# One pair of low matmuls behind the next six, in the down products and behind the mixer's totals

## The chip, the cores and the metric

One Trainium2 chip, one of its cores. The metric is the device time of one execution in microseconds (us); a median of three runs is given. TensorE is called PE, its weight loads PEld, VectorE DVE, ScalarE ACT, GpSimd POOL, and the queue that starts most loads SP.

## What is computed

One step of an encoder layer over T = 576 tokens (512 of a prompt and 64 of a running stream), with a model width of 1024 and an FFN width of 2816, all in fp32:

```python
x = x + 0.5 * swiglu_ffn(rms_norm(x, ffn1_norm), ffn1_w_gate_up, ffn1_w_down)
h = rms_norm(x, mix_norm)
p = h @ w_in                                  # 1024 -> 7168
y_a = (a_b * dwconv3(a_c * a_v)) @ w_a_out
y_b = silu(layer_norm(dwconv31(glu(b_u)) + bias)) @ w_b_out
x = x + (sigmoid(gate_a) * y_a + sigmoid(gate_b) * y_b) @ w_out
x = x + 0.5 * swiglu_ffn(rms_norm(x, ffn2_norm), ffn2_w_gate_up, ffn2_w_down)
y = rms_norm(x, final_norm)
```

The last inputs of the two convolutions are returned too.

## The kernel before

Features lie on the 128 partitions and the 576 tokens along the free dimension, so a product's output tile is 128 features by two halves of 288 tokens, each half in a PSUM bank of its own. Each fp32 operand is split into a high part (fp32r) and a low part, the rounded rest. A product of 128 input features (one *chunk*) is then three products, high x high, high x low, low x high, on two halves: six matmuls. `mm` (line 396) issues them in the order of `SIX`: four with the chunk's high weights (half 0, half 0, half 1, half 1), then two with its low weights (half 0, half 1). Each matmul comes with a weight load of 128x128.

```python
SIX = ((0, 0), (1, 0), (0, 1), (1, 1), (2, 0), (2, 1))

parts = ((whi, xh), (whi, xl), (wlo, xh))
```

Instructions of each engine are kept in the order in which the program issues them. Stages, in order:

- **First FFN.** Its 22 rows of gate and up tiles come in four groups of 5, 5, 6 and 6 (`GROUPS`). A first few rows are plain products; the others are *pairs* of seven *blocks* (`block`, line 417), each 12 matmuls into one bank. Behind each group stand its down products: eight output tiles `j`, each over the group's rows as chunks. Tiles 0 and 1 run together, chunk by chunk (`both`, line 470), tiles 2 to 7 one behind the other (`product`, line 444). In the last group `finish1` does this.
- **Mixer.** 56 products of `w_in` and 8 of `w_a_out`, `w_b_out` and `w_out` each, of 8 chunks (48 matmuls). Sums over features (RMSNorm, LayerNorm) are made by matmuls with a tile of ones: `Sum.total`, called a *total*, has four, a high and a low term on each half. There is one behind the mixer's first product, one for LayerNorm's mean, and one for its variance.
- **Second FFN.** As the first, with one total behind its first gate product. Of its last group only tiles 0 to 2 are made as above; tiles 3 to 7 (the *late* ones) are made over the first 304 tokens, then over the other 272, three matmuls a chunk.

Weights come in fp32 by SP. ACT rounds them to the high part, and a POOL DMA that adds makes the low part from the raw tile; for some tiles DVE subtracts instead. A weight tile's buffers come free when PE has used it.

The change adds a function `turn` beside `mm` and a flag `turned`, and touches `product`, `both` and `total`.

Of the kernel before, what the change touches and what calls it, by code (L numbers as in the profile page):

```python
# [56 lines left out]
SIX = ((0, 0), (1, 0), (0, 1), (1, 1), (2, 0), (2, 1))  # L57
# [49 lines left out]
def tile_encoder_step(  # L107
# [25 lines left out]
    def nm(s):  # L133
        uid[0] += 1
        return f"{s}_{uid[0]}"
# [16 lines left out]
    def psum2():  # L152
        return mmps.tile([P, 2, 512], F32, tag="mm", name=nm("mm"))
# [41 lines left out]
    class Stream:  # L195
# [91 lines left out]
        def lead(self, n, ahead=None):  # L287

            self.load_ahead()
            n, total = n + (ahead or self.ahead), len(self.units)  # L290
            while self.done < min(total, self.begun, n):
                self.end()
            while self.added < min(total, n + 2):
                self.add()
            while self.begun < min(total, n + 1):
                self.begin()
# [99 lines left out]
    def mm(ps, w, kk, xs, first, last, spans=HALVES, six=SIX):  # L396


        (whi, wlo), (xh, xl) = w, xs
        parts = ((whi, xh), (whi, xl), (wlo, xh))  # L400
        for n, s in six:
            if s < len(spans):
                (a, b), (i, e) = parts[n], spans[s]
                pe.matmul(
                    ps[:, s, : e - i], a[:, kk, :], b[:, i:e],
                    start=first and n == 0, stop=last and n == 2,
                )

    def chunks(name):

        got = []
        for n in plan[name]:
            w = ws.get(n)
            got += [(w, kk) for kk in range(ws.units[n][1])]
        return got

    def block(w, xs):
# [5 lines left out]
                pe.matmul(q, l[:, k, :], r, start=k == m == 0, stop=k == KU - 1 and m == 2)  # L423
        return q


    work = []

# [2 lines left out]
    def fill():  # L431
        while work and dve.time < pe.time - AHEAD:
            work.pop(0)()

    def take():

        while behind:
            ready, then = behind.pop(0)
            dve.time = max(dve.time, ready)
            then()  # L440
# [3 lines left out]
    def product(name, xs, then=None, order=None, got=None, soon=None):  # L444


        if name in early:
            return early.pop(name)[:, :, :H]
        ps = psum2()
        if order or got:  # L450
            got = got or chunks(name)
            for n, k in enumerate(order or range(len(xs))):
                mm(ps, *got[k], xs[k], n == 0, n == len(xs) - 1)
        else:
            k = 0
            for n in plan[name]:
                w = ws.get(n)
                for kk in range(ws.units[n][1]):
                    mm(ps, w, kk, xs[k], k == 0, k == len(xs) - 1)
                    k += 1  # L460
                    if soon and k == 1:
                        soon()
        take()
        if then is None:
            dve.time = max(dve.time, pe.time)
            return ps[:, :, :H]
        fill()
        behind.append((pe.time, lambda: then(ps[:, :, :H])))

    def both(names, xs):  # L470

        ps = [psum2() for _ in names]
        ws_ = [chunks(name) for name in names]
        for k in range(len(xs)):
            for p, w in zip(ps, ws_):
                mm(p, *w[k], xs[k], k == 0, k == len(xs) - 1)
        return [p[:, :, :H] for p in ps]
# [24 lines left out]
    class Sum:  # L502
# [49 lines left out]
        def total(self, spans=HALVES, room=None):  # L552

            if room:
                n = T // len(room)
                for s, out in enumerate(room):
                    for one, v in self.terms:
                        pe.matmul(
                            out, one, v[:, s * n : (s + 1) * n],
                            start=v is self.terms[0][1], stop=v is self.terms[-1][1],  # L560
                        )
                return room
            p = psum2()
            span = slice(spans[0][0], spans[-1][1])
            terms = self.terms or [(ones, self.acc[:, span]), (ones, self.last)]
            for s, (i, e) in enumerate(spans):
                for n, (one, v) in enumerate(terms):
                    pe.matmul(
                        p[:, s, : e - i], one, v[:, i - span.start : e - span.start],
                        start=n == 0, stop=n == 1,  # L570
                    )
            n = spans[0][1] - spans[0][0]
            return p[:, :, :n] if len(spans) == 2 else p[:, 0, :n]
# [190 lines left out]
    ws.ahead = 2  # L764
    name = ("f1", "u", 1)
    ps = product(name, xg, soon=root)
    early[name] = ps

# [10 lines left out]
    def ffn(f, xg, sums, finish, forms, R=None, todo=()):  # L779
# [5 lines left out]
        def plain(i, hs):  # L785
            nonlocal R
            t, up = ttile(), (f, "u", i)
            ps = product((f, "g", i), xg, order=IN_TURN if f == "f2" and i == 0 else None)
            got = None if up in early else chunks(up)
            if R is None:  # L790
                R = rstd(sums)
            ups = product(up, xg, got=got)
            hs.append(None)
            at = len(hs) - 1
# [73 lines left out]
        for g, grp in enumerate(GROUPS):  # L868
            hs = []
            for i in grp:  # L870
                if i < PLAIN[f]:
                    plain(i, hs)
                    continue
                if i == PLAIN[f]:
                    ws.ahead = AHEAD_UNITS
                    bs = forms.operands(xg)
                pair(i, hs, grp[-1] == FT - 1)
            while rest:
                rest.pop(0)()
            spare.clear()  # L880
            if grp[-1] < FT - 1:
                for j, ps in enumerate(both([(f, "d", g, j) for j in range(2)], hs)):
                    update(j, ps, R)
                for j in range(2, KT):
                    update(j, product((f, "d", g, j), hs), R)
            else:
                finish(g, hs)

    def finish1(g, hs):
        table(AF.Abs_reciprocal_sqrt)  # L890
        ps = both([("f1", "d", g, j) for j in range(2)], hs)
        for j in range(KT):
            update(j, ps[j] if j < 2 else product(("f1", "d", g, j), hs))
            nxg.append(split_scaled(X[j], par(j, R_NM)))
            nss.square(X[j])
            nss.add(dve)
# [115 lines left out]
    for j in range(KT):  # L1012
        raw = j < RAW_J
        xs = xg if raw else xn
# [142 lines left out]
    for j in range(KT):  # L1157
        ps = product(("yb", j), BA)
# [8 lines left out]
    for n, j in enumerate(IN_TURN):  # L1167
        ps = product(("o", j), MS)
# [4 lines left out]
        p = n // 2  # L1173
# [12 lines left out]
    def finish2(g, hs):  # L1186
        fsum = Sum()
        table(AF.Abs_reciprocal_sqrt)
        ps = both([("f2", "d", g, j) for j in range(2)], hs)
        for j in range(LATE[0]):  # L1190
            update(j, ps[j] if j < 2 else product(("f2", "d", g, j), hs))
# [121 lines left out]
```

## Time and profile before

| | us |
|---|---|
| median of three runs | 1294.79 |
| lowest, highest | 1294.35, 1294.93 |
| the profiled execution | 1294.93 |
| its span, first to last instruction | 1293.2 |
| PE busy in it | 1283.2 |

The profile is of one execution. A busy time is the union of instructions, and matmuls overlap: each lasts some 290 ns from start to modelled end, and the next starts some 130 ns after it did. A row of the timeline is a run of like instructions: its start, its length up to the end of the last, and how many; the start of the next row less its own start is the time that its matmuls took. Where a helper records every operation all have one line (L83), so stages are told apart by time and by names of tiles.

### The profile page before, as it was taken

What the parts mean: (1) busy time and instruction counts of PE and PEld (TensorE: products, weight loads), DVE (VectorE), ACT (ScalarE), POOL (GpSimd) and SP (SyncE); (2) the same over time, 40 slices, a digit from 0 to 9 for tenths busy, and PEclk for the clock granted to TensorE, in tenths of its full rate; (3) what the DMA queues carried; (4) which work ended last, traced back from release to release, by engine and by line L of the source; (5) the groups of instructions that cost most, each with busy time, mean ns of one, the idle gap of its engine ahead of it and who ended that gap; (6) DMA issues with size and microseconds to landing.
All of it is one profiled execution on the core that took longest, in us unless ns stands there. A gap on an engine that the chain in (4) does not pass through costs nothing.

```text
span 1293.2 us, 25663 instructions
## 1 busy us (share of the span) xinstructions
PE 1283.2 (99%) x9752; PEld 1281.8 (99%) x9752; DVE 893.0 (69%) x1477; ACT 763.5 (59%) x1353; POOL 370.2 (29%) x470
## 2 busy tenths in 40 slices
PE   9999999999999999999999999999999999999997
PEld 9999999999999999999999999999999999999997
DVE  6858668748846998898885160346857858847956
ACT  7646656645776655555454674467665655654664
POOL 0032322322333444333321322222142241241230
PEclk9999999999999999999999999999999999999999
DMA  7286786886799898787885978776697696796683
GB/s 223 66 187 150 164 183 148 178 178 152 153 196 186 172 204 167 171 170 171 175 170 121 206 158 167 168 158 140 139 176 175 149 197 148 160 209 135 160 173 93
DMA packets 285948, 213.16 MB, mean 165 GB/s; under 512 B 15360, under 2 KB 248832, under 8 KB 285824
## 3 DMA queue, kind: packets, MB, share of 16 engines
q0 software_dynamic: 57600, 95.05, 44.7%
q1 hardware_dynamic: 226480, 115.63, 31.4%
q8 instruction: 77, 1.26, 0.4%
q10 hardware_dynamic: 1744, 0.83, 0.2%
q14 instruction: 47, 0.39, 0.1%
HBM read 113.81 MB, written 2.62 MB: 90 GB/s over the span
## 4 chain that ended last, share of the span: by engine, by line
PE 88%; issue 8%; DMA 2%; POOL 1%; DVE 1%; ACT 0%; POOLq 0%; DVEq 0%; SPq 0%; ACTq 0%
PE mm L83 88%; DMA u<-raw 1%; POOL g L83 1%; POOL u L83 1%; DMA raw<-in_ffn_w_gate_up_dram 0%; DMA raw<-in_ffn_w_down_dram 0%; DMA g<-raw 0%; DVE g L83 0%; DVE tmp L83 0%; POOLq L83 0%; DVE w L83 0%; DVEq L1303 0%; ACT g L83 0%; ACT u L83 0%; DVE r L83 0%
## 5 line engine op out<-in xcount | busy, mean ns | idle before, releaser
L83 PE MATMUL mm<-act,u 128*128 128x288 f32 x4686 | 660.3, 293 | 0.2 <-DMA u<-raw 0.2
L83 PEld LDWEIGHTS mm<-act,u 128*128 128x128 f32 x4686 | 630.7, 188 | 0.4 <-DMA u<-raw 0.4
L83 PE MATMUL mm<-act,g 128*128 128x288 f32 x2778 | 399.2, 294 | 0.0
L83 PEld LDWEIGHTS mm<-act,g 128*128 128x128 f32 x2778 | 377.9, 188 | 0.0
L83 PE MATMUL mm<-act,act 128*128 128x288 f32 (+2 forms) x2244 | 306.1, 293 | 0.0
L83 PEld LDWEIGHTS mm<-act,act 128*128 128x128 f32 x2244 | 297.4, 188 | 0.3 <-ACT act L83 0.3
L83 POOL DMA_DIRECT2D u<-raw x197 | 171.7, 871 | 411.3 <-ACT u L83 300.8
L83 ACT CAST u<-raw 128x512 fp32r<-128x512 f32 (+2 forms) x203 | 116.2, 572 | 155.8 <-PE mm L83 127.3
L83 POOL DMA_DIRECT2D g<-raw x117 | 101.9, 871 | 274.4 <-ACT g L83 220.0
L83 DVE SCALAR_TENSOR_TENSOR w<-g,prm,w 128x606 f32<-128x606 f32 x232 | 179.2, 842 | 1.4 <-ACT w L83 1.4
L83 DVE TENSOR_TENSOR tmp<-mm,tmp 128x288 f32<-128x288 f32 (+1 forms) x239 | 107.4, 458 | 68.1 <-PE mm L83 53.1
L83 POOL DMA_DIRECT2D act<-raw x86 | 73.9, 859 | 195.5 <-ACT act L83 186.3
L83 ACT ACTIVATE u<-u 128x512 fp32r<-128x512 f32 (+2 forms) x197 | 116.9, 593 | 6.3
L83 DVE SCALAR_TENSOR_TENSOR tmp<-mm,r 128x576 f32<-128x576 f32 x48 | 36.3, 756 | 79.1 <-PE mm L83 79.1
L83 ACT CAST g<-raw 128x512 fp32r<-128x512 f32 (+2 forms) x126 | 68.9, 547 | 37.2 <-DMA raw<-in_ffn_w_down_dram 16.7
L83 ACT CAST u<-w 128x512 fp32r<-128x512 f32 x79 | 48.9, 619 | 63.1 <-DVE w L83 55.4
L83 ACT CAST g<-w 128x512 fp32r<-128x512 f32 x77 | 47.7, 619 | 61.6 <-DVE w L83 55.5
L83 ACT CAST act<-tmp 128x576 fp32r<-128x576 f32 x84 | 56.7, 675 | 42.7 <-DVE tmp L83 41.1
L83 DVE TENSOR_TENSOR act<-tmp,act 128x576 fp32r<-128x576 f32 x84 | 62.1, 754 | 18.2 <-ACT act L83 16.5
L83 ACT ACTIVATE g<-g 128x512 fp32r<-128x512 f32 (+2 forms) x117 | 66.4, 568 | 3.7
L83 ACT CAST act<-raw 128x512 fp32r<-128x512 f32 (+3 forms) x94 | 55.4, 592 | 12.1 <-PE mm L83 6.5
L83 DVE TENSOR_TENSOR w<-raw,raw 128x512 f32<-128x512 f32 x78 | 53.4, 684 | 10.0 <-DMA raw<-in_ffn_w_gate_up_dram 10.0
(88 smaller groups left out, 802.0 us busy)
## 6 DMA issues: line engine op xcount, KB each, us to landing
raw<-in_ffn_w_gate_up_dram SPq DMA_DIRECT2D x171, 256.0 KB, 3.4
u<-raw POOLq DMA_DIRECT2D x140, 256.0 KB, 4.0
raw<-in_w_in_dram SPq DMA_DIRECT2D x112, 256.0 KB, 3.6
act<-raw POOLq DMA_DIRECT2D x80, 256.0 KB, 4.2
raw<-in_ffn_w_down_dram SPq DMA_DIRECT2D x96, 192.0 KB, 3.6
g<-raw POOLq DMA_DIRECT2D x60, 256.0 KB, 3.8
g<-raw POOLq DMA_DIRECT2D x43, 192.0 KB, 4.4
u<-raw POOLq DMA_DIRECT2D x41, 192.0 KB, 4.4
```

The costliest lines, as they stand in the source:

```text
L83: return self.tc.keep_in_program_order(fn(*args, **kwargs))
```

## The change

A function `turn` issues two chunks' twelve matmuls in another order: four high ones of the first, all six of the second, and then the first one's two low ones. `both` uses it once, for chunk 1 of its two tiles. `product` uses it for its chunks 1 and 2, and only in the first product behind a total that is called without `room`; a product that takes its chunks from a list (`order` or `got`) resets the flag without using it, which is the case behind the second FFN's total. So there are eight places in `both` (four groups of each FFN) and three behind totals, and the same matmuls as before. Sums of a tile are added up in another order at these places.

```diff
+    def turn(tiles, xs):
+        (p, w, k, x), (q, v, l, z) = ((*t, x) for t, x in zip(tiles, xs))
+        for ps, u, kk, b, six in (p, w, k, x, SIX[:4]), (q, v, l, z, SIX), (p, w, k, x, SIX[4:]):
+            mm(ps, u, kk, b, False, False, six=six)
+
+    turned = [False]
...
     def product(name, xs, then=None, order=None, got=None, soon=None):
...
         ps = psum2()
+        at, turned[0] = 1 if turned[0] else None, False
...
                 for kk in range(ws.units[n][1]):
-                    mm(ps, w, kk, xs[k], k == 0, k == len(xs) - 1)
+                    if k == at:
+                        turn([(ps, w, kk), (ps, w, kk + 1)], xs[k : k + 2])
+                    elif at is None or k != at + 1:
+                        mm(ps, w, kk, xs[k], k == 0, k == len(xs) - 1)
...
     def both(names, xs):
...
         for k in range(len(xs)):
+            if k == 1:
+                turn([(p, *w[k]) for p, w in zip(ps, ws_)], [xs[k]] * 2)
+                continue
             for p, w in zip(ps, ws_):
                 mm(p, *w[k], xs[k], k == 0, k == len(xs) - 1)
...
             p = psum2()
+            turned[0] = True
             span = slice(spans[0][0], spans[-1][1])
```

How PE's instructions stand, first in the down products of the first FFN's first group, chunk 1 of tiles 0 and 1 (`mm` are the PSUM tiles; 1014 is tile 0 and 1015 tile 1; of the `u` pairs the first is the high part, the second the low one; x2 is both halves; "..." stands where rows that stay are left out):

```order
 L83 MATMUL mm_1014<-act_560,u_886 128x288
 L83 MATMUL mm_1014<-act_566,u_886 128x288
-L83 MATMUL mm_1014<-act_560,u_887 128x288 x2
 L83 MATMUL mm_1015<-act_560,u_925 128x288
 L83 MATMUL mm_1015<-act_566,u_925 128x288
...
 L83 MATMUL mm_1015<-act_566,u_925 128x288
 L83 MATMUL mm_1015<-act_560,u_926 128x288 x2
+L83 MATMUL mm_1014<-act_560,u_887 128x288 x2
 L83 MATMUL mm_1014<-act_708,u_886 128x288
 L83 MATMUL mm_1014<-act_714,u_886 128x288
```

Tile 0's two low matmuls moved from ahead of tile 1's six to behind them, so that eight matmuls with high weights and then four with low ones follow each other.

Then the first product behind the mixer's first total, chunks 1 and 2 of one PSUM tile (weights `act_5185` high, `act_5186` low; the second chunk's moving tiles are `act_5000` and `act_5001`):

```order
 L83 MATMUL mm_5402<-act_4941,act_5185 128x288
 L83 MATMUL mm_5402<-act_4942,act_5185 128x288
-L83 MATMUL mm_5402<-act_4941,act_5186 128x288 x2
 L83 MATMUL mm_5402<-act_5000,act_5185 128x288
 L83 MATMUL mm_5402<-act_5001,act_5185 128x288
...
 L83 MATMUL mm_5402<-act_5001,act_5185 128x288
 L83 MATMUL mm_5402<-act_5000,act_5186 128x288 x2
+L83 MATMUL mm_5402<-act_4941,act_5186 128x288 x2
 L83 MATMUL mm_5402<-act_5059,act_5185 128x288
 L83 MATMUL mm_5402<-act_5060,act_5185 128x288
```

Chunk 1's two low matmuls moved behind chunk 2's six. The same is done behind the second and third total, and in the other seven pairs of down tiles; DVE, ACT, POOL and SP issue what they did, in the same order.

## Rows read from the trace of the kernel before

**Rows 1.** The page: busy time, chain, costliest group of PE.

```profile
PE 1283.2 (99%) x9752; PEld 1281.8 (99%) x9752; DVE 893.0 (69%) x1477; ACT 763.5 (59%) x1353; POOL 370.2 (29%) x470
PE 88%; issue 8%; DMA 2%; POOL 1%; DVE 1%; ACT 0%; POOLq 0%; DVEq 0%; SPq 0%; ACTq 0%
L83 PE MATMUL mm<-act,u 128*128 128x288 f32 x4686 | 660.3, 293 | 0.2 <-DMA u<-raw 0.2
```

**Rows 2.** Timeline of PE around the mixer's first total: start, length, instruction, count.

```profile
395.57 3.32 PE L83 MATMUL mm<-act,act 128*128 128x288 f32 x24
...
401.90 0.69 PE L83 MATMUL mm<-tmp,ones_r 128*128 128x288 f32 x4
402.43 3.28 PE L83 MATMUL mm<-act,act 128*128 128x288 f32 x24
405.55 3.28 PE L83 MATMUL mm<-act,u 128*128 128x288 f32 x24
```

**Rows 3.** Timeline of PE: first matmuls of down groups, and of what follows them.

```profile
99.09 1.61 PE L83 MATMUL mm<-act,u 128*128 128x288 f32 x11
...
154.70 4.90 PE L83 MATMUL mm<-act,g 128*128 128x288 f32 x36
...
186.29 1.74 PE L83 MATMUL mm<-act,g 128*128 128x288 f32 x12
...
357.66 1.61 PE L83 MATMUL mm<-act,g 128*128 128x288 f32 x11
...
1139.87 1.34 PE L83 MATMUL mm<-act,u 128*128 128x288 f32 x9
...
1177.79 1.74 PE L83 MATMUL mm<-act,u 128*128 128x288 f32 x12
```

**Rows 4.** Windows: PE, PEld, DVE, ACT, POOL busy; then PEclk, DMA share, GB/s.

```profile
155.00:186.00 31.00, 31.00 (x237) 31.00 (x237) 16.69 (x24) 14.89 (x31) 10.91 (x13) 1.00 0.92 196
402.50:687.00 284.50, 284.50 (x2191) 284.50 (x2189) 249.19 (x381) 151.67 (x246) 104.88 (x157) 1.00 0.83 173
```

**Rows 5.** Timeline of PE around the second and third total.

```profile
689.47 0.69 PE L83 MATMUL mm<-tmp,ones_r 128*128 128x288 f32 x4
690.00 3.32 PE L83 MATMUL mm<-act,act 128*128 128x288 f32 x24
...
715.28 0.69 PE L83 MATMUL mm<-tmp,ones_r 128*128 128x288 f32 x4
715.81 3.28 PE L83 MATMUL mm<-act,act 128*128 128x288 f32 x24
```

**Rows 6.** Timeline of PE around the second FFN's total.

```profile
903.02 0.69 PE L83 MATMUL mm<-tmp,ones_r 128*128 128x288 f32 x4
903.55 3.32 PE L83 MATMUL mm<-act,g 128*128 128x288 f32 x24
906.71 3.32 PE L83 MATMUL mm<-act,u 128*128 128x288 f32 x24
```

**Rows 7.** Timeline of PE around the first FFN's total of six short matmuls.

```profile
24.89 0.81 PE L83 MATMUL mm<-tmp,ones_r 128*128 128x192 f32 x6
25.53 2.56 PE L83 MATMUL mm<-act,g 128*128 128x288 f32 x18
27.93 2.27 PE L83 MATMUL mm<-act,u 128*128 128x288 f32 x16
```

**Rows 8.** Timeline of PE in the last down group: a wait for data.

```profile
1246.18 3.70 PE L83 MATMUL mm<-act,u 128*128 128x288 f32 x26 [0.19 <-DMA u<-raw]
```

**Rows 9.** Timeline of PE in the late tiles, around their total.

```profile
1271.59 2.82 PE L83 MATMUL mm<-act,act 128*128 128x272 f32 x21
1274.25 0.47 PE L83 MATMUL mm<-tmp,ones_r 128*128 128x304 f32 x2
1274.56 8.68 PE L83 MATMUL mm<-act,act 128*128 128x272 f32 x69
1283.08 0.62 PE L83 MATMUL mm<-acc,ones 128*128 128x272 f32 x2
```

## The prediction

> **What bounds the kernel now.** I read the page first: TensorE (PE) is busy for 1283.2 us, 99% of the span, and 88% of the chain that ended last are its matmuls [rows 1]. So the time is a number of matmuls times their spacing, and an order of matmuls can matter only through the spacing. Next I read the timeline of PE, because the duration of one (293 ns [rows 1]) overlaps with its neighbours'; only starts tell the spacing. The reader is to divide the distance of two starts by the matmuls between them.
>
> In the mixer, 24 matmuls start every 3.12 us: 130.0 ns each [rows 2]. In the down products of the first FFN, 240 matmuls take 186.29 - 154.70 = 31.59 us, which is 131.6 ns, and the last group's 288 take 37.91 us (from 357.66 to 395.57), again 131.6 [rows 2, 3]. A group of the second FFN says the same: 37.92 us for 288 [rows 3]. All are 128x288 matmuls, each with a load of 128x128 of one type, in the same six-step pattern, and the granted clock is 1.00 (the 2.4 GHz level) in the fast stretch and in the slow ones [rows 4]. So the same work has two paces, **1.66 ns apart per matmul**, and holds one for hundreds of matmuls.
>
> What changes the pace? The rows show it at the totals. The mixer's first product is slow (48 matmuls from 395.57 to 401.90, 131.8 each), four matmuls with ones follow at 401.90, and from 402.43 on the pace is 130.0 [rows 2]. It stays so for 2208 matmuls, to 689.47 (287.04 us, 130.0 each); four matmuls of the next total, and 192 matmuls take 25.28 us, 131.7 each, to 715.28; four more, and 1440 take 187.21 us from 715.81 on, 130.0 each [rows 5, 6]. The total of the second FFN turns it slow once more: 3.16 us for 24 from 903.55 on [rows 6]. Four totals of four, four changes, two in each direction. A total of six short matmuls at 24.89 left the pace slow: the 18 behind it took 2.40 us [rows 7].
>
> **The change, part by part.** No instruction is added or removed, only two low matmuls per place move behind six others, and the order of the other four engines is the same. There are 11 places: eight pairs of down tiles and the product behind each of three totals. Any gain must come from the pace.
>
> What a place does to the pace, no row shows: this order does not occur before. The nearest row is a total. It sets four matmuls with one weight tile ahead of four with another, where otherwise two with a low part stand between. The change begins in the same way (four of p, four of q), and then sets two low pairs behind each other. My reading is that the four behind four is what moves the pace, as at four totals of four. Against it: the total's weights are another tile (ones), and the second half of the change could undo the first. So the effect on a place lies between 0 and a full change of pace; I take the full change, because the total is the nearest row, and keep the zero for the range.
>
> With it, the terms are (each place loses the matmuls ahead of the new order and the twelve in it: 24 at a pair, 18 behind a total):
> - Down, first FFN: groups of 5, 5, 6, 6 rows x 8 tiles x 6 = 1056 matmuls, less 4 x 24 = 960, x 1.66 ns = -1.59 us.
> - Down, second FFN: groups of 5, 5, 6 give 768, the last group's first three tiles 108; 876 - 96 = 780 x 1.66 = -1.29 us.
> - The mixer's first product, now slow [rows 2]: 48 x 1.66 = -0.08 us.
> - Between the second and third total 192 matmuls are slow (25.28 us [rows 5]): 174 x 1.66 = -0.29 us.
> - At the first and third total the pace is fast today by the total alone. With a fast pace ahead of it, the total makes it slow (as at 689.47) and the new order brings it back 18 matmuls later: 2 x 18 x 1.66 = +0.06 us.
> - The second FFN's total is followed by a product that takes its chunks from a list, which has no new order: slow there now, slow after. Nothing.
> - The late tiles: 21 matmuls of 272 columns take 2.66 us ahead of their total (126.7 ns) and 69 take 8.52 us behind it (123.5) [rows 9]. If the pace comes in fast, that total turns it the wrong way: -0.07 + 0.23 = +0.16 us. For the 304-column ones no other pace is shown, so I take nothing; one as large as 1.66 ns would be 0.15 us for their 90.
>
> Sum: -1.59 - 1.29 - 0.08 - 0.29 + 0.06 + 0.16 = **-3.03 us**. The profiled execution took 1294.93 us (span 1293.2 and 1.7 around it), 0.14 above the median of the three runs; 1294.79 - 3.03 = 1291.8.
>
> Do the other engines keep up when PE gains 1.3% in these stretches? DMA engines are busy for 0.92 of their time in one of them [rows 4], but PE shows one wait for data in all down products: 0.19 us of idle time ended by a low part's transfer at 1246.18 [rows 8]. What fills the weights is itself released by PE as buffers come free, so I expect the wait to move along. If it does not move, it eats what is gained behind the last release, at most the group before it: 264 x 1.66 = 0.44 us. That is one end of my own case, 1292.2. The other end is without the 0.16 of the late tiles and with 0.15 at 304 columns: 1291.5.
>
> A rule that speaks against all this: the Trainium skill, TensorE: Matmul & The Clock Gate, section Back-to-back issue gap, gives the gap of matmuls as a function of their columns alone, N/2.4 + 2.5 ns at full clock. By it the order could do nothing and the sum would be 0. The trace does not agree: it has 130.0 and 131.6 ns for one form [rows 2, 3].
>
> **Rivals.**
> - *Nothing happens.* The second half of the new order undoes the first (two low pairs back to back mirror two high fours), or it is the weights with ones that change the pace. For: six matmuls with ones moved nothing [rows 7], so not every insertion works. Against: two with ones inside the late tiles go with a change from 126.7 to 123.5 [rows 9], so the count is not peculiar. Time: 1294.8, within 0.2. The page's rule above gives the same.
> - *Some groups only.* The pace depends on what stood ahead of it, and half of the eight groups change: about half of the sum, 1293.3.
> - *Slower: the new order changes the pace each time, and the blocks between two down groups keep what they were given.* Then down groups alternate, fast, slow, fast, slow, and the first FFN ends slow. The first total makes the pace fast, and the new order behind it makes it slow: (2208 - 18) x 1.66 = +3.64 us in the mixer. The second total makes it fast and the order slow, as today. The third the same: (1440 - 18) x 1.66 = +2.36 us (1440 matmuls from 715.81 to 903.02 [rows 5, 6]). Kept of the gain: 480 matmuls of the first FFN and some 300 of the second, -1.30 us. Sum +4.7, 1299.5; blocks that go fast could take 2 us off it. It is decided by one thing: whether the pace is fast when PE reaches 401.90. For: no row shows blocks entered at the fast pace. Against: blocks have a pace of their own (99.09 to 154.70 us for 420 matmuls, 132.4 ns [rows 3]), and every down group behind them begins slow.
> - *Blocks gain too.* They keep the fast pace and go at 130.0: 34 pairs x 84 x 2.4 ns = 6.9 us more, 1285. Same evidence, and then the alternation above would more likely follow.
>
> **How the numbers follow.** My forecast 0.50, nothing 0.23, some groups 0.10, slower 0.13, blocks too 0.04. The measurement can tell about 0.2%, 2.6 us, from no change; my 3.0 is only just beyond. So faster is 0.44 of my own 0.50, all of the blocks, and a little of the partial case: 0.50. Same: 0.06 + 0.08 + 0.22 = 0.36. Slower: 0.14. The range takes in my case with its ends and half a microsecond for the unknown start of the blocks below them, the partial case and the zero: 1290.6 to 1295.2. Left out are the slower case and the blocks, 0.17.
>
> **What would show it.** In the timeline after: 240 down matmuls in 31.3 us instead of 31.59, 288 in 37.5 instead of 37.9, the stretch between the second and third total 25.0 instead of 25.28, and the mixer still 287.0 from the first total to the second. Nothing happened if these stand as before. The slower case is a mixer of 290.7. I am wrong on the terms if the late tiles do not trade places or if the wait at 1246.18 grows.

## The result, and the profile after

| | before | after |
|---|---|---|
| median, us | 1294.82 (9 runs) | 1298.31 (9 runs) |
| lowest, highest | 1294.35, 1295.55 | 1297.38, 1298.98 |
| the profiled execution, us | 1294.93 | 1298.06 |
| its span | 1293.2 | 1296.3 |

The ratio is 1.0027, with a 95% interval of 1.0019 to 1.0035: 3.5 us slower. The forecast was 1291.8, its range 1290.6 to 1295.2. The two profiled executions differ by 3.13 us; all that follows splits these.

The page of the profile doesn't say where the time went: PE is busy for 3.0 us more, with the same number of instructions and much the same chain, to be compared with [rows 1].

```profile
PE 1286.2 (99%) x9752; PEld 1284.9 (99%) x9752; DVE 893.6 (69%) x1477; ACT 763.4 (59%) x1353; POOL 370.4 (29%) x470
...
PE 87%; issue 8%; DMA 2%; POOL 1%; DVE 1%; ACT 0%; POOLq 0%; DVEq 0%; SPq 0%; ACTq 0%
...
L83 PE MATMUL mm<-act,u 128*128 128x288 f32 x4686 | 662.2, 294 | 0.1
```

The timeline of PE at the down groups (start, length, instruction, count), to be compared with [rows 3]:

```profile
154.20 4.90 PE L83 MATMUL mm<-act,g 128*128 128x288 f32 x36
...
185.46 1.74 PE L83 MATMUL mm<-act,g 128*128 128x288 f32 x12
...
356.38 1.88 PE L83 MATMUL mm<-act,g 128*128 128x288 f32 x13
...
393.88 1.47 PE L83 MATMUL mm<-act,act 128*128 128x288 f32 x10
...
1143.54 1.75 PE L83 MATMUL mm<-act,u 128*128 128x288 f32 x12
...
1181.04 1.74 PE L83 MATMUL mm<-act,u 128*128 128x288 f32 x12
```

The groups of 240 now take 185.46 - 154.20 = 31.26 us (31.59 before), those of 288 take 37.50 (37.9): these down products have the fast pace, as forecast. The same view at the four totals, to be compared with [rows 2, 5, 6]:

```profile
400.13 0.69 PE L83 MATMUL mm<-tmp,ones_r 128*128 128x288 f32 x4
400.66 3.34 PE L83 MATMUL mm<-act,act 128*128 128x288 f32 x24
403.84 3.33 PE L83 MATMUL mm<-act,u 128*128 128x288 f32 x24
...
691.40 0.69 PE L83 MATMUL mm<-tmp,ones_r 128*128 128x288 f32 x4
691.93 3.34 PE L83 MATMUL mm<-act,act 128*128 128x288 f32 x24
...
717.23 0.69 PE L83 MATMUL mm<-tmp,ones_r 128*128 128x288 f32 x4
717.77 3.34 PE L83 MATMUL mm<-act,act 128*128 128x288 f32 x24
...
907.39 0.69 PE L83 MATMUL mm<-tmp,ones_r 128*128 128x288 f32 x4
907.92 3.32 PE L83 MATMUL mm<-act,g 128*128 128x288 f32 x24
911.08 1.08 PE L83 MATMUL mm<-act,u 128*128 128x288 f32 x7
```

From the first total's end to the second total, 2208 matmuls take 691.40 - 400.66 = 290.74 us, 131.7 ns each (287.04 before). From the second to the third, 192 take 25.30 (25.28). From the third to the second FFN's total, 1440 take 189.62 (187.21). The new order stands behind three of these totals, and the pace behind each is slow. The clock has no part in it; windows of the mixer (PE, PEld, DVE, ACT, POOL busy; PEclk, DMA share, GB/s) give 1.00, as [rows 4], with 2163 matmuls in a stretch that held 2191:

```profile
402.50:687.00 284.50, 284.50 (x2163) 284.50 (x2162) 248.49 (x380) 151.03 (x245) 103.13 (x154) 1.00 0.81 171
```

The last down group and the late tiles, before and after, to be compared with [rows 8, 9]. First the kernel before:

```profile
1244.51 1.48 PE L83 MATMUL mm<-act,u 128*128 128x288 f32 x10
...
1249.71 4.90 PE L83 MATMUL mm<-act,g 128*128 128x288 f32 x36
...
1259.19 3.06 PE L83 MATMUL mm<-act,act 128*128 128x304 f32 x21
```

Then the changed one:

```profile
1247.75 5.25 PE L83 MATMUL mm<-act,u 128*128 128x288 f32 x36
1252.84 4.90 PE L83 MATMUL mm<-act,g 128*128 128x288 f32 x36
...
1262.32 2.92 PE L83 MATMUL mm<-act,act 128*128 128x304 f32 x20
...
1274.72 2.82 PE L83 MATMUL mm<-act,act 128*128 128x272 f32 x21
...
1277.38 0.47 PE L83 MATMUL mm<-tmp,ones_r 128*128 128x304 f32 x2
1277.68 8.68 PE L83 MATMUL mm<-act,act 128*128 128x272 f32 x69
1286.20 0.62 PE L83 MATMUL mm<-acc,ones 128*128 128x272 f32 x2
```

The group's first 36 take 5.09 us (5.20 before), against 4.74 for 36 at 131.7: the wait for data got shorter but did not go, though the view shows no idle time now. The other 72 take 1262.32 - 1252.84 = 9.48 us, as they did before (1259.19 - 1249.71 = 9.48), 131.7 ns each: this group did not get the fast pace. The late tiles go as before, 2.66 us for 21 and 8.52 for 69.

The whole program, from start to start, after less before (us):

| stretch | matmuls | forecast | measured |
|---|---|---|---|
| start, up to the first down group | 490 | 0 | -0.14 |
| downs of the first FFN | 1056 | -1.59 | -1.53 |
| blocks between them | 1428 | 0 | -0.02 |
| mixer's first product | 48 | -0.08 | -0.08 |
| first total, and the product behind it | 52 | +0.03 | +0.11 |
| mixer, up to the second total | 2160 | 0 | **+3.59** |
| second total to third | 196 | -0.29 | +0.02 |
| third total to the second FFN's | 1444 | +0.03 | **+2.42** |
| downs of the second FFN, three groups | 768 | -1.15 | -1.11 |
| the second FFN's total, product and blocks | 1816 | 0 | -0.02 |
| last group's first three tiles | 108 | -0.14 | -0.12 |
| late tiles | 185 | +0.16 | 0.00 |
| sum | | -3.03 | +3.12 |

The forecast of the second FFN's downs (-1.29) is split here by the matmuls behind each place. The -0.12 of the last group is the shorter wait, none of it pace. So the question for the runs was why one order ends the slow pace at seven down groups and not behind the three totals.

### The profile page after: what moved, and what is told of

It is laid out like the page before. It is cut to its first block, busy times and chain, and to the rows that moved or that the text cites. A ratio compares the mean times of both kernels' runs of the same rounds, so it can differ in the third digit from the quotient of the medians.

```text
span 1296.3 us, 25663 instructions
## 1 busy us (share of the span) xinstructions
PE 1286.2 (99%) x9752; PEld 1284.9 (99%) x9752; DVE 893.6 (69%) x1477; ACT 763.4 (59%) x1353; POOL 370.4 (29%) x470
## 4 chain that ended last, share of the span: by engine, by line
PE 87%; issue 8%; DMA 2%; POOL 1%; DVE 1%; ACT 0%; POOLq 0%; DVEq 0%; SPq 0%; ACTq 0%
PE mm L83 87%; POOL g L83 1%; DMA u<-raw 1%; POOL u L83 1%; DMA raw<-in_ffn_w_gate_up_dram 0%; DMA raw<-in_ffn_w_down_dram 0%; DMA g<-raw 0%; DMA gains<-in_params_dram 0%; DVE g L83 0%; DVE tmp L83 0%; POOLq L83 0%; DVE w L83 0%; ACT act L83 0%; DVEq L1321 0%; ACT g L83 0%
```

## What the starts say, and the two theories

A row of the timeline rounds to 10 ns. The starts themselves are in whole ns, and the distance from each start to the next, chunk by chunk (six matmuls a line), shows what the rows can't. Around the first total:

```
before
  last chunk ahead    132 131 130 131 134 135   slow, long half
  four with ones      139 127 132 129
  chunk 0             128 132 131 133 130 126   fast
after
  last chunk ahead    128 132 131 133 130 131   fast
  four with ones      134 137 129 132
  chunk 0             130 134 127 134 132 133   slow, short half
  turn, first six     131 131 131 131 134 133   begins on the long half
  turn, last six      138 132 132 131 131 140
  chunk 3             131 130 139 133 132 130
  chunk 4             132 133 133 136 126 131
after, down group at 154.20
  turn, first six     128 133 132 134 132 136   begins on the short half
  turn, last six      136 136 135 134 130 126
  next                128 132 130 134 130 126   fast
```

The fast pace repeats every chunk (780 ns a chunk). The slow one repeats only **every second chunk**: 131 133 128 133 133 132, which I call the short half for its step of 128 (126 to 128), then 132 131 130 131 134 132, the long half; 790 ns each. (Where the slow pace has just set in, as at 154.20, the short step stands first in its half; later, third.) In seven of the eight down groups the new order begins behind two chunks (one of each tile), on the short half, and the pace behind it is fast. In the eighth, the last of the second FFN, PE is held up just ahead of it, at the matmul at which the kernel before waits for data (steps of 374 and 238 ns), the next six go at the fast pace (129 131 131 133 130 128), and the new order, begun on that pace, makes it slow. Behind the first total it begins behind one chunk, on the long half, and the pace stays slow.

- **Theory "half":** the turn ends the slow pace if it begins on the short half; on the long half it only shifts the halves by one chunk. A total behind a long half makes a slow pace fast (before: first and third), behind a short half it leaves it slow (after: second, third and the second FFN's), and a fast pace it makes slow.
- **Rival "tiles":** the turn works where its two chunks belong to two PSUM tiles, as in the downs, and not within one tile.

## Experiments

The first was timed in 11 runs. For the others there is one execution each, the profiled one; the kernel before took 1294.7 to 1295.3 beside them.

**e1_chunk2: the turn behind a total one chunk later.**

```diff
-        at, turned[0] = 1 if turned[0] else None, False
+        at, turned[0] = 2 if turned[0] else None, False
```

> The new order behind the mixer's totals starts at chunk 2 instead of chunk 1; the down pairs keep theirs. Theory 'half' (the slow pace repeats after twelve matmuls, so it has two halves of six, and the order ends it only when it starts on the first of them, which chunk 0 behind a total is and chunk 1 is not): the mixer is fast again, 287.1 us from its first total to the second, 25.1 between the second and third, 187.3 from the third to the second FFN's total; time 1291.8 us. Rival 'tiles' (the order works only with two PSUM tiles that share a chunk's moving data, as in the down pairs): the mixer stays slow as in the changed kernel, 290.7, 25.3 and 189.6 us; time 1298.3 us.

Measured: 1292.17 us (1291.11 to 1293.14, 11 runs) against 1294.76, ratio 0.9979 (0.9970 to 0.9988). The windows of the mixer and the timeline at the second and third total:

```profile
402.50:687.00 284.50, 284.50 (x2190) 284.50 (x2190) 248.71 (x381) 151.10 (x245) 104.08 (x154) 1.00 0.83 174
```

```profile
688.09 0.69 PE L83 MATMUL mm<-tmp,ones_r 128*128 128x288 f32 x4
688.62 3.33 PE L83 MATMUL mm<-act,act 128*128 128x288 f32 x24
...
713.63 0.69 PE L83 MATMUL mm<-tmp,ones_r 128*128 128x288 f32 x4
714.17 3.33 PE L83 MATMUL mm<-act,act 128*128 128x288 f32 x24
```

The mixer is fast again: 2190 matmuls where the changed kernel has 2163. Between the second and third total 192 take 25.01 us, the 25.0 that I had forecast. The first 24 behind a total take 3.17 us (12 slow ones, then the twelve of the turn). The turn within one tile does end the slow pace, one chunk later than the change has it: "half" holds, "tiles" falls. This version is faster than both kernels. In its profile it is 3.31 us below the kernel before; -0.59 of that is the last group of the second FFN, where the wait for data is gone (-0.47 in the first 36) and the turn, which then meets the slow pace, ends it (-0.12 in the other 72). The order alone doesn't do that: e8, with the same order, has the wait again (14.69 us for the 108, as before). The rows of e1 there:

```profile
1241.78 4.90 PE L83 MATMUL mm<-act,u 128*128 128x288 f32 x36
1246.52 4.84 PE L83 MATMUL mm<-act,g 128*128 128x288 f32 x36
```

**e2_downs_alone: no turn behind totals.**

```diff
             p = psum2()
-            turned[0] = True
```

> The new order in the eight down pairs alone, none behind totals. Theory 'half': the first total is met at the fast pace and makes it slow (mixer 290.7 us to the second total); the second total is met behind the second half of the slow pace and makes it fast (192 matmuls in 24.96 us), the third makes it slow (189.6 us), the second FFN's total makes it fast for one product (48 matmuls in 6.24 us); time 1297.6 us. Rival 'tiles' says the same of the first stretch and nothing of where the later totals leave the pace: if a total met at the slow pace makes it fast whatever the half, the same as 'half'; if the totals of the changed kernel are the rule (slow stays slow), 25.3, 189.6 and 6.32 us and 1298.2 us.

Measured: 1298.47 us. The timeline at the second, third and the second FFN's total:

```profile
692.27 0.69 PE L83 MATMUL mm<-tmp,ones_r 128*128 128x288 f32 x4
692.79 3.28 PE L83 MATMUL mm<-act,act 128*128 128x288 f32 x24
...
717.76 0.69 PE L83 MATMUL mm<-tmp,ones_r 128*128 128x288 f32 x4
718.29 3.32 PE L83 MATMUL mm<-act,act 128*128 128x288 f32 x24
...
908.42 3.28 PE L83 MATMUL mm<-act,g 128*128 128x288 f32 x24
911.54 0.42 PE L83 MATMUL mm<-act,u 128*128 128x288 f32 x2
```

The mixer is slow as in the changed kernel (+3.60 us), so what makes it slow is the first total, met at the fast pace that the downs now hand on. With no turn to shift the halves, the second total comes behind a long half and makes the pace fast (717.76 - 692.79 = 24.97 us for 192), the third makes it slow (+2.40), the last fast (3.12 us for 24, where before and the changed kernel have 3.16). All four came as "half" orders them; the time is 0.9 us above the expected 1297.6, 0.74 of it ahead of the first down group.

**e3_totals_alone: no turn in the downs.**

```diff
-            if k == 1:
-                turn([(p, *w[k]) for p, w in zip(ps, ws_)], [xs[k]] * 2)
-                continue
```

> The new order behind the three totals alone, none in the down pairs. Down groups as before the change (31.6 and 37.9 us). The first total is met slow, as before the change, and makes the pace fast; then the order starts at the fast pace, which no run has shown. If it leaves a fast pace alone, the first mixer stretch takes 287.0 us, and with theory 'half' the second total makes it slow, the order at chunk 1 leaves it slow, and the third total is met behind a first half and leaves it slow (189.6 us): 1297.2 us. If it ends a fast pace too, the first stretch takes 290.7 us and the time is 1298 to 1301 us. Rival 'tiles': the order does nothing in one tile, so 287.0 us, and the rest as before the change but for the totals: 1294.8 to 1297.2 us.

Measured: 1301.09 us. The timeline behind the first total, and the window of the mixer:

```profile
402.12 0.69 PE L83 MATMUL mm<-tmp,ones_r 128*128 128x288 f32 x4
402.64 3.31 PE L83 MATMUL mm<-act,act 128*128 128x288 f32 x24
405.78 3.33 PE L83 MATMUL mm<-act,u 128*128 128x288 f32 x24
```

```profile
402.50:687.00 284.50, 284.50 (x2163) 284.50 (x2162) 248.58 (x380) 150.29 (x244) 103.23 (x155) 1.00 0.82 172
```

The downs are slow as before, so the total meets the slow pace and makes it fast: chunk 0 goes at 780 ns. Then the turn, begun at the fast pace, makes it slow (3.14 us for the first 24, then 3.16), +3.59 us up to the second total. So behind the first total the turn as it stands helps in neither run: here it ends the fast pace, in the changed kernel it leaves the slow one.

**e4_pair_other_half: in the downs, the turn one chunk later.** It now takes tile 1's chunk 1 and tile 0's chunk 2, still two tiles.

```diff
             if k == 1:
-                turn([(p, *w[k]) for p, w in zip(ps, ws_)], [xs[k]] * 2)
+                mm(ps[0], *ws_[0][1], xs[1], False, False)
+                turn([(ps[1], *ws_[1][1]), (ps[0], *ws_[0][2])], xs[1:3])
+                mm(ps[1], *ws_[1][2], xs[2], False, False)
+            if k in (1, 2):
                 continue
```

> In the down pairs the new order starts one group of six later: tile 1's chunk 1 and tile 0's chunk 2, two PSUM tiles but the second half of the slow pace; behind totals as in the changed kernel. Theory 'half': the down groups stay slow, 31.6 us for 240 matmuls and 37.9 for 288, and the mixer too; time about 1301 us. Rival 'tiles': the two tiles are what counts, the down groups are fast, 31.26 and 37.5 us; time 1298.3 us. (It also has two moving tiles where the changed kernel's pair has one: if that is what counts, slow as with 'half', and the run at chunk 2 behind totals, which has two as well, tells the two apart.)

Measured: 1300.89 us. The timeline at the second down group:

```profile
154.63 2.54 PE L83 MATMUL mm<-act,g 128*128 128x288 f32 x18
...
186.26 1.74 PE L83 MATMUL mm<-act,g 128*128 128x288 f32 x12
```

240 matmuls in 31.63 us: slow, although two tiles take part. The steps of this turn are those of the changed kernel's behind its first total, within 2 ns: 132 131 131 131 134 133, then 138 132 132 131 131 140. With e1 this is the other half of the proof: moved by one chunk, the turn in one tile starts to work and the turn in two tiles stops. Nor is it the number of moving tiles: both of these turns have two, and one works. The mixer is slow too, though PE reaches the first total at the slow pace: the total comes behind a short half here and leaves it slow.

**e5_before_pad32 and e6_before_pad64: is it the places of the operands?** The blocks hint at it: their matmuls have the shape of the others, and go at 131.7 ns on moving half 0 and 133.4 on half 1, whose tokens lie 1152 B further. Both runs have PE's order of the kernel before. A tile of 32 B (`n` = 8; in e6 64 B, `n` = 16) moves every operand but the tile of ones.

```diff
     X = [cpool.tile([P, T], F32, tag=f"x{j}", name=f"x{j}") for j in range(KT)]
+    pad = cpool.tile([P, n], F32, tag="pad", name="pad")
+    pool.memset(pad, 0.0)
```

> The kernel before, with a tile of 32 B set behind x in SBUF, so that every weight, activation and scratch tile begins 32 B later (at a multiple of 64 B, where in the kernel before it begins 32 B past one; the tile of ones stays where it is, at such a multiple). PE's order is that of the kernel before. Theory 'address' (the spacing of matmuls depends on where the operands begin, as the blocks' 131.7 ns on moving half 0 and 133.4 ns on half 1 suggest): the mixer's 130.0 ns a matmul falls or rises by 0.5 ns or more, the down products' 131.6 change too, the time moves by 5 us or more (9752 matmuls x 0.5 ns). Rival 'address does not matter': mixer 130.0, down 131.6, between the second and third total 25.28 us, 1294.8 us.

> The same with a tile of 64 B: all tiles but the ones begin 64 B later, still 32 B past a multiple of 64 B. Theory 'address', if it is the place within 64 B that counts: as the kernel before, 1294.8 us, mixer 130.0 and down 131.6 ns. If a larger unit counts: a change of the size of the run with 32 B. Rival 'address does not matter': 1294.8 us.

Measured: 1300.86 us with 32 B, 1295.09 with 64. Windows of the mixer, of e5 and of e6:

```profile
402.50:687.00 284.50, 284.50 (x2163) 284.50 (x2162) 248.41 (x380) 149.89 (x244) 103.26 (x155) 1.00 0.80 172
719.90:900.00 180.10, 180.10 (x1370) 180.10 (x1369) 63.81 (x94) 108.81 (x176) 50.02 (x58) 1.00 0.79 171
```

```profile
402.50:687.00 284.50, 284.50 (x2191) 284.50 (x2190) 249.20 (x381) 151.77 (x246) 105.17 (x157) 1.00 0.82 174
```

The run with 32 B fits neither expectation. In it the paces themselves are unchanged (downs and blocks to 1 ns in a group, the mixer 131.67), so a shift by 32 B does not set them. But the first total, reached behind a long half as in the kernel before, no longer makes the pace fast, nor do the other three totals of four: 2163 and 1370 matmuls in the two windows. With 64 B the pace of every stretch is as before. So what a *total* does changes with a shift by 32 B and not with one by 64; whether that is the place of the ones against the other tiles or the place of the other tiles alone, these runs don't tell. The rule on totals above holds for one placement.

**e8_chunk2_pad32 and e9_after_pad32: does the turn depend on it too?** The kernel of e1 and the changed kernel, with the 32 B.

> The kernel with the turn at chunks 2 and 3 behind a total (that of e1_chunk2), and all tiles but the ones 32 B later. In e5_before_pad32 the totals left PE slow, and behind its first total the first two chunks passed through other steps before the half with the short step began at chunk 2. Theory 'half' (the turn in chunks of one tile needs no tile of ones, so the 32 B change nothing for it): down groups fast (31.26 us per 240), and behind the first total, if it is reached fast and leaves the halves as in e5, the turn at chunk 2 begins on the half with the short step: mixer 130.0, time near 1292. Rival 'place': the turn too works by where its tiles lie against each other and the ones: down groups 31.6 and mixer 131.67, 1300.9 as in e5.

> The changed kernel, all tiles but the ones 32 B later. Theory 'half': down groups fast as in the changed kernel (31.26 us per 240, no tile of ones takes part); behind a total the turn at chunk 1 begins on the half without the short step and leaves PE slow, 131.67 in the mixer, 1298.3. Rival 'place': down groups 31.6 and 1300.9; or the total met fast leaves it fast and the turn ends that: 1298 as well, but with chunk 0 at 130.0.

Measured: 1291.89 us for e8, 1298.18 for e9. The timeline of e8 at the second down group and its window of the mixer, then the window of e9:

```profile
154.35 4.90 PE L83 MATMUL mm<-act,g 128*128 128x288 f32 x36
...
185.60 1.08 PE L83 MATMUL mm<-act,g 128*128 128x288 f32 x7
```

```profile
402.50:687.00 284.50, 284.50 (x2191) 284.50 (x2190) 248.57 (x380) 150.98 (x245) 104.28 (x154) 1.00 0.81 173
```

```profile
402.50:687.00 284.50, 284.50 (x2163) 284.50 (x2162) 248.88 (x381) 150.97 (x245) 102.91 (x153) 1.00 0.80 172
```

The turn works alike in both placements: downs fast (185.60 - 154.35 = 31.25 us in e8), the mixer fast with the turn at chunk 2 and slow with it at chunk 1. A total met at the fast pace makes it slow here too: chunk 0 of e9 takes steps of 132 130 139 132 132 131, not those of the fast pace, so the rival's second case did not happen either. The next three totals of e9 come behind a short half and leave the pace slow. With 32 B, then, all of the totals of four, behind either half and at either pace (e5, e8, e9), left it slow.

## Why the prediction was wrong

**What held.** Nearly all that moved is PE's spacing; the rest is the start (-0.14) and the shorter wait (-0.12). The terms of seven down groups were right in sign and size (-1.53 for -1.59; -1.11 for -1.15), and so was the mixer's first product (-0.08). The last group's -0.12 for -0.14 is luck: its pace did not change, and the wait, which was forecast to move along, got shorter. The argument against the alternation held too: blocks have a pace of their own, and every down group behind them begins slow. The other engines kept up, and the wait at 1246.18 did not grow.

**The step that failed** is the sentence "I take the full change, because the total is the nearest row", where it covers the three places behind totals. Its case was "four totals of four", and with it the term "the new order brings it back 18 matmuls later", +0.06 us. The order brought nothing back: behind the first and the third total the pace stayed slow for the whole stretch, +3.59 and +2.42 us, and behind the second the -0.29 came as +0.02. Whether the order ends the slow pace hangs on the half of the two-chunk pattern on which it begins (e1 and e4), and that is short in the downs and long behind these totals. "Four totals, four changes" was the same mistake: in this kernel a total met slow has two outcomes, and before's first and third both came behind a long half. The same goes for the row that was read as "left the pace slow", the total of six short matmuls: in five of the ten runs it made the pace fast (last section). The pattern could have been read beforehand: it stands in the starts of the kernel before, below what a row that rounds to 10 ns shows.

**The slower rival** had the places and the prices: a mixer of 290.7 us (290.74) and +2.36 behind the third total (+2.42). What it said decides did happen, the pace was fast when PE reached the first total, but it is not what decides: in e3 and e4 the pace was slow there, and the mixer was slow all the same (284.40 us for 2160 in each). Its way there was wrong too. Blocks kept no pace, the first FFN's last down group begins slow and ends fast by the turn alone, the first total made the pace slow and the turn merely failed to mend it. e2 shows this apart: without any turn behind totals the time is the same within 0.4 us, 1298.47. Its 4.7 us came out as 3.1 because the groups did not alternate, and seven of eight kept their gain.

**Late tiles.** The +0.16 did not come: the last down group leaves PE slow, so its condition was not met, and the 272-column ones reach their total at 126.6 ns and leave it at 123.5, as before. In e1 it was met: they reach it at 123.4 (21 in 2.59 us) and leave it at 123.5, so that total did not turn a fast pace round.

**The rule from the skill.** I read the Trainium skill's TensorE: Matmul & The Clock Gate, section Back-to-back issue gap, for its gap by columns. That section calls the formula the gap of an isolated matmul, and says that in a stream of loads and matmuls the spacing is set by both together, so the formula was not meant for a stream such as this one; no run here separates loads from matmuls. Neither statement knows an order, and in these runs the order alone moved the time from 2.6 us below the kernel before to 6.3 above it (e1, e3).

**What stays open.** What in the chip holds one of two paces over thousands of matmuls isn't shown; nor why a shift by 32 B changes what a total does, which one pair of placements shows and no more. In these runs a turn that begins on a short half also begins an even number of chunks behind the start of its stage, and none has the one without the other; the last down group (and e3) shows only that the place alone isn't enough, since the same place, met at the fast pace, ends slow. The runs show the rule for this pattern of six and for 288 columns.

## What to carry to other kernels

When identical instructions run at two paces, look at single starts before summing up: the slow pace may have a longer period than the loop, and an order that ends it in one phase leaves it alone in the other. An order that makes one stretch fast also changes the state in which the next is entered; here, behind stretches that won 1.6 us, two totals that used to leave the mixer fast left it slow, and that cost 6.0 us. Try such a change at both phases (here, one chunk later) before giving it up: the same edit moved by one chunk went from 3.5 us slower to 2.6 us faster.

## What the runs showed that was not expected

- 128x288 matmuls, each with its own 128x128 load, hold 130.00 or 131.67 ns for up to 2160 matmuls, with granted clock 1.00 and no waits in either; the slow pace repeats after 12 matmuls, the fast one after 6.
- Moving PE's operands, all but the ones, by 32 B changed the time of a program with the same order by 6.2 us (1300.86 against 1294.7), moving them by 64 B by 0.4, one execution each.
- PE's order is the same in all ten runs up to the first down group, and yet the last 330 matmuls ahead of it (matmuls 160 to 490) take 43.4 us in five (before, after, e2, e6, e8) and 43.0 in five (e1, e3, e4, e5, e9). The first FFN's total of six short matmuls stands there, and it too has two outcomes. With the tiles as in the kernel before or 64 B later it made the pace fast behind a short half (e1, e3, e4) and left it slow behind a long one (before, after, e6); with 32 B it was the other way round (fast behind a long half in e5 and e9, slow behind a short one in e8). In e2 it came behind steps of neither half and left the pace slow. Which half it meets differs from run to run, and so does the time of the 160 matmuls ahead, 22.95 to 23.83 us; that the one comes of the other isn't shown. The blocks behind end either pace.
